# A two-layer mixer kernel on one core: the low parts of its weight blocks made by accumulating transfers

## The chip, the core and the metric

The kernel runs on one core of one Trainium2 chip. The metric is the time of one execution on the device, in microseconds (us). The kernel before has a median of 2033.26 us over two runs (2032.23 and 2034.3).

## What is computed

Two mixer layers work on 512 latent tokens and 256 context tokens with 1024 features. Each layer normalizes, scales and shifts its input, projects it with one wide weight matrix, runs two branches of eight heads (retention, and mLSTM with a matrix memory), merges them by sigmoid gates, projects once more and adds the result to its input. Cut to what matters here:

```
for l in range(DEPTH):
    hx = rmsnorm(x, norm_w) * (1 + sc_x) + sh_x            # hc the same way from ctx
    u  = einsum('bld,de->ble', h, w_in) + b_in             # rq rk rv rz mq mk mv mo mz mg gr gm
    br = einsum('ble,ed->bld', yr, w_ret_o)                # yr: head norm of retention, gated
    bm = einsum('ble,ed->bld', ym, w_ml_o)                 # ym: head norm of mLSTM, gated
    y  = sigmoid(gr) * br + sigmoid(gm) * bm
    x  = x + g_x * einsum('bld,de->ble', y, w_out)         # ctx too, in the first layer only
return rmsnorm(x, final_norm_w)
```

All weights and activations are float32. The second layer computes only the latent tokens behind its heads' keys and values.

## The kernel before

Activations lie transposed, features on the partitions and tokens on the free axis. Every large projection splits both operands into a high part, which is the value rounded to float32r, and a low part, which is the remainder, and sums three products in PSUM: high times high, high times low of the activation, and low of the weight times high. TensorE (PE) thus reads the low part of a weight block in every third matmul, the first of them being the third matmul of a group.

Weights come as blocks of 1024 by 128 numbers, kept as a tile of 128 partitions by 1024 numbers (512 KB). `specs` lists the units of work in order; a unit is two blocks, except for the unit `rvg` of each layer, which comes in three pieces. `wload` (L171) prepares a unit: for each block `rawtile` (L164) issues a load into one of three buffers of the tag `raw` on the queue of SP, and `split` (L160) writes the high part with ScalarE (ACT, L161) and the low part with VectorE (DVE, L162), which subtracts the high part from the raw block:

```
s.activation(dh, src, AF.Copy)
(eng or v).tensor_tensor(dl, src, dh.bitcast(F32), op=OP.subtract)
```

High and low parts lie in the tiles `wh` and `wl`, with two buffers each. `nextw` (L190) hands out the unit that is wanted and prepares the next one. A unit can be prepared only into the buffers of the unit before the one that PE works on, so its time is what PE needs for one unit. Both layers together have 124 units in 250 pieces: 121 pieces in the first layer, 129 in the second. `split` has other users, which the change leaves alone: the start parameters (`ada`), the normalized activations `h`, the branch results `yr`, `ym` and the merged `y`.

How long a unit lasts on PE depends on its place. In the first layer a unit of two blocks multiplies 512 latent and 256 context columns; in the second layer most multiply the 512 latent ones alone. The short units are these: in the output projection `ou` (L1081, `mm3`), which takes the tokens in two passes and loads all weights again for the second, the second pass of the first layer and both passes of the second handle 256 columns; and in the second layer the units `mv` (L980, `mvc`) of the mLSTM heads handle the 256 context tokens, each between a unit `mz` and the unit `vo` of an odd head (1, 3, 5, 7).

GpSimd (POOL) does elementwise work and issues a few stores: the rope sum (L654), products with row tables (L695, L822, L806), small fills (L762, L772, L781 to L785), a power for each norm (L377, L623), squares and products of the norms (L366, L386), and the stores of `yrd`, `ymd` (L636) and `gmd` (L996) to DRAM. The kernel is built with a scheduler that orders the instructions of each engine by its own estimate of times; every engine then runs its list in that order and waits at each instruction for what it needs.

Of the kernel before, what the change touches and what calls it, by code (L numbers as in the profile page):

```python
"""Two mixer layers (bidirectional retention and mLSTM branches) on one core.

Activations are kept transposed (features on partitions, tokens on the free axis,
context tokens first).  The large projections split each float32 operand into a
float32r part and its float32r remainder and sum three products in PSUM; the
attention products run in plain float32.
"""
# [1 line left out]

# [7 lines left out]
AF = mybir.ActivationFunctionType  # L17
OP = mybir.AluOpType
PSUM = bass.MemoryType.PSUM
# [40 lines left out]
def build(tc, io):  # L60
# [3 lines left out]
    with ExitStack() as es:  # L64
# [10 lines left out]
        v, s, g, pe = nc.vector, nc.scalar, nc.gpsimd, nc.tensor  # L75

        def stage(name, dt=F32):
            return stp.tile([P, 774], dt, tag="st", bufs=6, name=name)
# [10 lines left out]
        def chunks(t, n=NCH):  # L89
            return t.rearrange("p (n c) -> p n c", n=n)  # L90

        # Work units are emitted in order; after each, every generator under way
        # gives up one stage, so that what a stage needs is ready when it comes.
        main, side = [], []

        def advance(q, gen):
# [24 lines left out]
                yield  # L121
            yield from gen

# [1 line left out]
        def const(name, shape):  # L125
            t = cst.tile(list(shape), F32, name="k_" + name)
            nc.sync.dma_start(t, io[name])
            return t
# [27 lines left out]
        nhalf = cst.tile([P, 1], F32, name="nhalf")  # L156
        g.memset(nhalf, -0.5)

# [1 line left out]
        def split(dh, dl, src, eng=None):  # L160
            s.activation(dh, src, AF.Copy)  # L161
            (eng or v).tensor_tensor(dl, src, dh.bitcast(F32), op=OP.subtract)  # L162

        def rawtile(src, name, shape=(KB, P)):  # L164
            raw = wp.tile([P, KB * P], F32, tag="raw", bufs=3, name="raw_" + name)
            raw = raw[:, :shape[0] * shape[1]].rearrange("p (k c) -> p k c", k=shape[0])
            nc.sync.dma_start(raw, src)
            return raw

        specs, loaded, wpos = [], {}, [0]  # L170
        def wload(i):  # L171
            if i >= len(specs) or i in loaded:
                return
            name, blocks = specs[i]
            wh = wp.tile([P, KB * VG], F32R, tag="wh", bufs=2, name="wh_" + name)
            wl = wp.tile([P, KB * VG], F32R, tag="wl", bufs=2, name="wl_" + name)
            if name.startswith("rvg"):
                wh, wl = [t.rearrange("p (k c) -> p k c", k=KB) for t in (wh, wl)]
                for a, b in ((0, 3), (3, 6), (6, 8)):
                    raw = rawtile(blocks[0][:, a:b], f"{name}_{a}", (b - a, VG))  # L180
                    split(wh[:, a:b], wl[:, a:b], raw)
                loaded[i] = (wh, wl)
                return
            wh, wl = [t[:, :2 * KB * P].rearrange("p (j k c) -> p j k c", j=2, k=KB) for t in (wh, wl)]
            for j, ap in enumerate(blocks):
                raw = rawtile(ap, f"{name}_{j}")
                split(wh[:, j], wl[:, j], raw)
            loaded[i] = (wh, wl)

        def nextw(ahead=True):  # L190
# [49 lines left out]
                              start=kb == 0 and sx is hp[0] and mv is w[0], stop=kb == KB - 1 and mv is w[1])  # L240
            return ps

# [1 line left out]
        sil = cst.tile([P, KB, 2], F32, name="sil")  # L244
        s.activation(sil, ccols, AF.Tanh, scale=0.5)
        v.scalar_tensor_tensor(sil, sil, 1.0, ccols, op0=OP.add, op1=OP.mult)
# [49 lines left out]
        def ada_first(kb):  # L296
            w = loaded["a", kb]
            ps = btile(f"ada_{kb}")
            if kb in NATSET:
                for j in range(2):  # L300
                    for k in range(KB):
                        pe.matmul(ps[:, j * P:(j + 1) * P], sils[:, k].bitcast(F32), w[j][:, k], start=k == 0,
                                  stop=k == KB - 1)
            else:
                for mv in w:
                    for k in range(KB):
                        pe.matmul(ps[:, :2 * P], sils[:, k], mv[:, :, k], start=k == 0 and mv is w[0],
                                  stop=k == KB - 1 and mv is w[1])
            return ps
# [47 lines left out]
                    accs[i] = acc  # L357
                yield

# [1 line left out]
        def square_add(acc, xk, k, sl, eng=None):  # L361
            t = stage(f"sq{k}") if k else acc
            if eng is None:
                s.activation(t[:, sl], xk[:, sl], AF.Square)
            else:
                eng.tensor_tensor(t[:, sl], xk[:, sl], xk[:, sl], op=OP.mult)  # L366
            if k:
                v.tensor_tensor(acc[:, sl], acc[:, sl], t[:, sl], op=OP.add)
# [28 lines left out]
                s.activation(t[:, sl], t[:, sl], AF.Identity, scale=sc, bias=b)  # L397
            split(hi, lo, t[:, sl], v if l else g)

# [1 line left out]
        wb = io["wblk"]  # L401

        def spec(name, *blocks):
# [24 lines left out]
                for p in range(4):  # L428
                    spec(f"{nm}{p}_{l}", io[nm][l, 2 * p], io[nm][l, 2 * p + 1])

# [1 line left out]
        rst = stage("rst_in")  # L432
        acc = stage("acc_in")
        hp = (big.tile([P, KB, T], F32R, tag="b0", name="h0_hi"), big.tile([P, KB, T], F32R, tag="b1", name="h0_lo"))
# [1 line left out]
        rows = {0: ada_first(0)}  # L436
# [41 lines left out]
        for l in range(NL):  # L478
# [29 lines left out]
            ymd = [dr.tile([P, T], F32, name=f"ymd{l}_{h}") for h in range(H)]  # L508
            gmd = [dr.tile([P, T], F32, name=f"gmd{l}_{j}") for j in range(KB)]

# [1 line left out]
            def gates(gtok):  # L512
                for a, b in ((0, 4), (4, 6)):
                    ps = btile(f"gtr{l}_{a}")
# [87 lines left out]
            def gate_rows(h):  # L602
                nc.sync.dma_start(gw[:, :, qsl], grow[h:h + 1][:, :, qsl].to_broadcast([P, 4, qsl.stop - qsl.start]))

# [1 line left out]
            def gate_z(pss, j, vb, hb, zT, name):  # L606
                t = stage(name)
                for ps, sl in pss:
                    s.activation(t[:, sl], ps, AF.Tanh, scale=0.5, bias=hv[:, hb + j:hb + j + 1])
                    s.activation(zT[:, sl], ps, AF.Identity, bias=vc[:, vb + j:vb + j + 1])  # L610
                v.scalar_tensor_tensor(zT[:, qsl], t[:, qsl], 1.0, zT[:, qsl], op0=OP.add, op1=OP.mult)
# [28 lines left out]
                nc.sync.dma_start(bt, io["brow"][l, idx:idx + 1, :].to_broadcast([P, VG]))  # L640
                return bt

# [1 line left out]
            def ret_v(w, bt, p, n0):  # L644
                vt = chunks(vts[p % 2][:, :1536])
                ps = projv(w, hp, n0, f"rv{l}_{p}_{n0}")
                v.tensor_tensor(vt[:, n0:n0 + 2], chunks(ps, 2), bt[:, None, :256].to_broadcast([P, 2, 256]), op=OP.add)
# [104 lines left out]
                finished.add(("r", l, h))  # L752
                yield

# [1 line left out]
            def ml_v(w, bt, h, n0):  # L756
                vt = chunks(vts[h % 2])
                ps = projv(w, hp, n0, f"mv{l}_{h}_{n0}")
# [131 lines left out]
                finished.add(("m", l, h))  # L890
                yield

# [1 line left out]
            if l == 0:  # L894
                late_consts()
            zet = sml.tile([P, 2, H], F32, tag="zet", bufs=1, name=f"zet{l}")
# [1 line left out]
            for p in range(4):  # L898
# [43 lines left out]
                for i in range(6):  # L942
                    h = 2 * p + i // 3
# [38 lines left out]
                main.append(ml_att(h))  # L982
                tick(False)

# [1 line left out]
            if l == 0:  # L986
                side.append(ada_rest(gw, ada_todo[ADAN:]))
            for p in range(4):
                w = nextw()
                for jj in range(2):  # L990
                    j = 2 * p + jj
# [17 lines left out]
            for p in range(4):  # L1009
                w = nextw()  # L1010
                for jj in range(2):
                    j = 2 * p + jj
# [5 lines left out]
                    tick(False)  # L1018
            drain(main)

# [1 line left out]
            for p in range(4):  # L1022
                w = nextw()
                for jj in range(2):
                    j = 2 * p + jj
# [10 lines left out]
            for p in range(4):  # L1036
                w = nextw()
                for jj in range(2):
                    j = 2 * p + jj
# [6 lines left out]
                    tick()  # L1046
            drain(side)

# [1 line left out]
            X = big.tile([P, KB, T], F32, tag="b2", name=f"X{l}")  # L1050
            for j in range(KB):
                nc.sync.dma_start(X[:, j, qsl], (io["xT"][j] if l == 0 else x1d[j])[:, qsl])
# [19 lines left out]
            for i, sl in enumerate((LAT, CTX) if need else (slice(256, 512), slice(512, 768))):  # L1072
                n = sl.stop - sl.start
                d = 1 if sl is CTX else 0
                for p in range(4):
                    w = nextw()
                    for jj in range(2):
                        j = 2 * p + jj
# [87 lines left out]
```

## Time and profile before

| what | value |
|---|---|
| median of the runs, lowest, highest | 2033.26 us, 2032.23 us, 2034.3 us |
| span of the profiled execution, first to last instruction | 2032.1 us |
| PE busy | 1990.1 us, 98% of the span |
| DVE busy | 1427.0 us, 70% |
| ACT busy | 718.9 us, 35% |
| POOL busy | 370.0 us, 18% |
| bytes moved by DMA | 229.59 MB, 113 GB/s in the mean |

The span of the profiled execution lies 1.2 us below the median of the runs. Busy times are times in which an engine works; matmuls are pipelined, so that a new one can start long before the one before it ends, and two starts 0.12 us apart are possible with matmuls of 0.28 us. Instructions that issue a transfer are not counted as busy time.

### The profile page before, as it was taken

How to read it: one execution, taken by the hardware profiler on the slowest of the kernel's cores; microseconds unless marked ns; L12 is line 12 of the kernel's file. 1: busy time of each engine (PE TensorE's matmuls, PEld its weight loads, DVE VectorE, ACT ScalarE, POOL GpSimd, SP SyncE). 2: the span in 40 equal slices, each digit the busy share in tenths (PEclk: the TensorE clock that was granted, in tenths of full speed). 3: DMA queues.
4: the chain of work that ended last, by engine and by line, in shares of the span. 5: the costliest groups of instructions: out<-in, count | busy, mean ns of one | idle time of the engine just before them, and what ended most of it. 6: DMA issues, size and time to landing. Idle time of an engine off the chain costs nothing.

```text
span 2032.1 us, 32593 instructions
## 1 busy us (share of the span) xinstructions
PE 1990.1 (98%) x12676; PEld 1799.9 (89%) x12676; DVE 1427.0 (70%) x3303; ACT 718.9 (35%) x1362; POOL 370.0 (18%) x431
## 2 busy tenths in 40 slices
PE   6989999999999999999999999999999999999997
PEld 6988989999999999888888888899899999988887
DVE  7886996566858585888834689655667886763356
ACT  5423222334434434343212442322334444434223
POOL 4312222221212121100000341312212122110000
PEclk9999999999999999999999999999999999999999
DMA  8213322212322323454524431222233333325435
GB/s 297 75 45 104 123 81 84 71 57 101 106 82 88 100 85 98 162 175 153 175 86 158 152 101 45 96 71 76 76 112 103 117 120 121 114 98 184 137 120 171
DMA packets 74716, 229.59 MB, mean 113 GB/s; under 512 B 8960, under 2 KB 17408, under 8 KB 73536
## 3 DMA queue, kind: packets, MB, share of 16 engines
q1 hardware_dynamic: 70464, 211.56, 32.0%
q0 software_dynamic: 4096, 15.93, 2.0%
q8 instruction: 100, 1.64, 0.3%
q14 instruction: 56, 0.46, 0.1%
HBM read 206.29 MB, written 21.17 MB: 112 GB/s over the span
## 4 chain that ended last, share of the span: by engine, by line
PE 87%; DVE 9%; issue 2%; DMA 1%; ACT 0%; POOL 0%; SPq 0%; POOLq 0%; DVEq 0%; ACTq 0%
PE mv L232 11%; PE mqk_l L216 9%; PE rqk_l L216 7%; PE bm_l L216 4%; PE gm_l L216 4%; PE br_l L216 4%; PE mz_l L216 4%; PE gr_l L216 4%; PE rv L232 4%; PE ou L205 4%; PE mqk_c L218 3%; PE rz_l L216 3%; PE rqk_c L218 2%; PE ro L743 2%; PE mo L869 2%
## 5 line engine op out<-in xcount | busy, mean ns | idle before, releaser
L232 PE MATMUL mv<-wh_vo,h_hi 128*128 128x256 f32 x640 | 183.6, 287 | 0.0
L232 PE MATMUL mv<-wl_vo,h_hi 128*128 128x256 f32 x640 | 183.2, 286 | 0.0
L232 PE MATMUL mv<-wh_vo,h_lo 128*128 128x256 f32 x640 | 182.0, 284 | 0.0
L356 DVE SCALAR_TENSOR_TENSOR aacc<-gw,sil,aacc 128x128 f32<-128x128 f32 x448 | 138.7, 362 | 0.0
L232 PEld LDWEIGHTS mv<-wh_vo,h_hi 128*128 128x128 f32 x640 | 122.6, 191 | 0.4
L232 PEld LDWEIGHTS mv<-wh_vo,h_lo 128*128 128x128 f32 x640 | 122.5, 191 | 0.2
L792 DVE SCALAR_TENSOR_TENSOR cv<-u,vec,cv 128x770 f32<-128x770 f32 (+1 forms) x128 | 121.3, 949 | 1.8
L232 PEld LDWEIGHTS mv<-wl_vo,h_hi 128*128 128x128 f32 x640 | 122.4, 191 | 0.0
L822 POOL TENSOR_TENSOR ws<-ws,gw 128x768 f32<-128x768 f32 (+1 forms) x32 | 53.3, 1686 | 321.5 <-PE mo L871 155.1
L216 PE MATMUL mqk_l<-h_lo,wh_mqk 128*128 128x512 f32 x256 | 103.8, 405 | 0.0
L216 PE MATMUL mqk_l<-h_hi,wh_mqk 128*128 128x512 f32 x256 | 103.3, 403 | 0.0
L216 PE MATMUL mqk_l<-h_hi,wl_mqk 128*128 128x512 f32 x256 | 102.4, 400 | 0.0
L654 POOL TENSOR_TENSOR ws<-ws,rp 128x512 f32<-128x512 f32 x32 | 52.6, 1644 | 189.6 <-DVE ws L653 149.6
L232 PE MATMUL rv<-wl_rv,h_hi 128*128 128x256 f32 x288 | 83.2, 289 | 0.0
L232 PE MATMUL rv<-wh_rv,h_hi 128*128 128x256 f32 x288 | 83.1, 289 | 0.0
L232 PE MATMUL rv<-wh_rv,h_lo 128*128 128x256 f32 x288 | 82.8, 288 | 0.0
L205 PE MATMUL ou<-yl,wh_wout 128*128 128x256 f32 (+1 forms) x256 | 79.1, 310 | 0.0
L205 PE MATMUL ou<-yh,wl_wout 128*128 128x256 f32 (+1 forms) x256 | 79.1, 310 | 0.0
L205 PE MATMUL ou<-yh,wh_wout 128*128 128x256 f32 (+1 forms) x256 | 78.7, 309 | 0.0
L743 PE MATMUL ro<-ws,ws 128*128 128x128 f32 x448 | 65.2, 279 | 9.5 <-DVE gsm L563 3.9
L695 POOL TENSOR_TENSOR ws<-ws,ws 128x768 f32<-128x768 f32 (+1 forms) x32 | 53.1, 1678 | 106.4 <-PE ro L743 106.2
L743 PEld LDWEIGHTS ro<-ws,ws 128*128 128x128 f32 x448 | 59.7, 194 | 12.8 <-DVE st L744 8.1
(444 smaller groups left out, 6536.2 us busy)
## 6 DMA issues: line engine op xcount, KB each, us to landing
gw<-in_wada SPq DMA_DIRECT2D x32, 512.0 KB, 3.4
raw_vo<-in_wblk SPq DMA_DIRECT2D x32, 512.0 KB, 4.2
raw_mqk<-in_wblk SPq DMA_DIRECT2D x32, 512.0 KB, 3.8
raw_wout<-in_wout SPq DMA_DIRECT2D x32, 512.0 KB, 3.9
gw<-grow SPq DMA_DIRECT2D x8, 1536.0 KB, 6.3
raw_qk<-in_wblk SPq DMA_DIRECT2D x16, 512.0 KB, 3.4
raw_zq<-in_wblk SPq DMA_DIRECT2D x16, 512.0 KB, 3.3
raw_kz<-in_wblk SPq DMA_DIRECT2D x16, 512.0 KB, 3.7
```

What stands on the lines that cost most here:

```text
L205: pe.matmul(dst, lw[:, j, kb], mv[:, kb, sl], start=first, stop=last)
L216: pe.matmul(lat, lw[:, j, kb], mv[:, kb, LAT], start=first, stop=last)
L218: pe.matmul(c[:, :NCTX], lw[:, j, kb], mv[:, kb, CTX], start=first, stop=last)
L232: pe.matmul(dst, sx[:, kb, tk], mv[:, :, kb], start=first, stop=last)
L356: v.scalar_tensor_tensor(o, raw[:, kb], sil[:, kb, d:d + 1], o, op0=OP.mult, op1=OP.add)
L654: g.tensor_tensor(dst[:, LAT], dst[:, LAT], t[:, :512], op=OP.add)
L695: g.tensor_tensor(chunks(qd[d][:, qsl], nq), chunks(qT[:, qsl], nq), xi[d][:, None, :].to_broadcast([P, nq, P]), op=OP.mult)
L743: pe.matmul(o, lt, rt, start=k == 0, stop=k == len(ops) - 1)
L792: v.scalar_tensor_tensor(y[:, o0:o0 + n], u[:, o0 + i:o0 + i + n], cw[i], y[:, o0:o0 + n], op0=OP.mult, op1=OP.add)
L822: g.tensor_tensor(qd[d][:, qsl], qT[:, qsl], gw[:, 2 + d, qsl], op=OP.mult)
L869: pe.matmul(o, ch(sT[d], n), vt[:, n, 0:129], start=True, stop=first)
```

## The change

A new helper `wsplit` takes the place of `split` for the 250 weight pieces. ACT writes the high part as before, and then writes the negative of the raw block, rounded in the same way, into the low tile. POOL's queue then issues a transfer that reads the same weight block from DRAM a second time and adds it to what lies in the low tile: the block less its high part is the low part. DVE has no part in it any more. The raw load stays.

```
+        def wsplit(dh, dl, raw, src):
+
+            s.activation(dh, raw, AF.Copy)
+            s.activation(dl, raw, AF.Copy, scale=-1.0)
+            g.dma_start(dl, src, accum_op=OP.add)
...
                     raw = rawtile(blocks[0][:, a:b], f"{name}_{a}", (b - a, VG))
-                    split(wh[:, a:b], wl[:, a:b], raw)
+                    wsplit(wh[:, a:b], wl[:, a:b], raw, blocks[0][:, a:b])
...
                 raw = rawtile(ap, f"{name}_{j}")
-                split(wh[:, j], wl[:, j], raw)
+                wsplit(wh[:, j], wl[:, j], raw, ap)
```

The rest of the diff takes comments out; code below the helper stands six lines lower than before, so POOL's L623 is L629 in the changed kernel, L806 is L812, and the transfer of the helper is L168.

The scheduler orders the changed program anew. On POOL in the second layer's mLSTM heads, before, the stretch behind the power of head 1's norm (`ve_m1_1`) reads:

```order
L822 TENSOR_TENSOR ws3_1_11584<-ws1_1_11582,gw1_11585 128x512 x2
L772 MEMSET ws2_1_11583 128x2
L623 TENSOR_TENSOR ve_m1_1_15305<-ve_m1_1_15305,nhalf_104 128x4
L762 MEMSET ws2_1_11583 128x2
L781 MEMSET u1_3_0_15596 128x2
L782 MEMSET u1_3_0_15596 128x2
L636 DMA ymd1_1_11598<-yo_m1_1_15407 128x512
```

The same stretch of POOL's list in the changed kernel, where `wl_mv2`, `wl_vo3` and `wl_mqk3` are the low tiles of three units that follow each other:

```order
L168 DMA wl_mv2_1_15377<-in_wblk 128x1024 x2
L828 TENSOR_TENSOR ws3_1_11708<-ws1_1_11706,gw1_11709 128x512 x2
L629 TENSOR_TENSOR ve_m1_1_15479<-ve_m1_1_15479,nhalf_104 128x4
L168 DMA wl_vo3_1_15519<-in_wblk 128x1024 x2
L778 MEMSET ws2_1_11707 128x2
L787 MEMSET u1_3_0_15776 128x2
L788 MEMSET u1_3_0_15776 128x2
L812 TENSOR_TENSOR ws3_1_11708<-gw1_11709,k_negm_510 128x512
L168 DMA wl_mqk3_1_15624<-in_wblk 128x1024
```

The transfers for `wl_vo3` now stand behind the power of head 1's norm, and those for `wl_mqk3` behind that and a table product.

On PE in the second layer's output projection, where `ou1_4_0` and `ou1_5_0` belong to the unit `wout2` and `ou1_6_0` to the unit after it, the changed kernel reads as follows, behind the last matmul of the unit `wout1`:

```order
L211 MATMUL ou1_4_0_19182<-yh1_18723,wh_wout2_1_19100 128x256
L211 MATMUL ou1_4_0_19182<-yl1_18724,wh_wout2_1_19100 128x256
L211 MATMUL ou1_5_0_19211<-yh1_18723,wh_wout2_1_19100 128x256
L211 MATMUL ou1_5_0_19211<-yl1_18724,wh_wout2_1_19100 128x256
L211 MATMUL ou1_6_0_19252<-yh1_18723,wh_wout3_1_19170 128x256
L211 MATMUL ou1_6_0_19252<-yl1_18724,wh_wout3_1_19170 128x256
```

Before, the matmul that reads the low tile stood third in the list, and each block's 24 matmuls followed each other:

```order
L205 MATMUL ou1_4_0_18940<-yh1_18495,wh_wout2_1_18862 128x256
L205 MATMUL ou1_4_0_18940<-yl1_18496,wh_wout2_1_18862 128x256
L205 MATMUL ou1_4_0_18940<-yh1_18495,wl_wout2_1_18863 128x256
L205 MATMUL ou1_4_0_18940<-yh1_18495,wh_wout2_1_18862 128x256
L205 MATMUL ou1_4_0_18940<-yl1_18496,wh_wout2_1_18862 128x256
```

The first two matmuls of four blocks, which need high parts alone, are thus put ahead of the first that reads a low tile.

## Rows read from the trace of the kernel before

**Rows 1.** Page, part 1: busy us, share of the span, instructions.

```profile
span 2032.1 us, 32593 instructions
PE 1990.1 (98%) x12676; PEld 1799.9 (89%) x12676; DVE 1427.0 (70%) x3303; ACT 718.9 (35%) x1362; POOL 370.0 (18%) x431
```

**Rows 2.** Waits of PE, longest first: us in total, times, longest.

```profile
PE ada L307 <- ACT wh_ada L161: 8.1, 1, 8.1
PE ro L743 <- DVE gsm L563: 3.9, 1, 3.9
...
PE rkv L709 <- DVE adx L340: 0.6, 1, 0.6
PE rkv L709 <- ACT ws L618: 0.3, 1, 0.3
```

**Rows 3.** Windows by stage: us, busy by engine, PE clock, DMA share, GB/s.

```profile
1140.00:1170.00 30.00, 28.12 (x229) 27.69 (x228) 22.40 (x24) 16.69 (x23) 16.31 (x11) 0.99 0.54 163
1460.00:1790.00 330.00, 329.71 (x2205) 303.05 (x2205) 242.48 (x578) 136.14 (x275) 58.21 (x109) 1.00 0.35 111
1790.00:1962.00 172.00, 172.00 (x792) 143.24 (x791) 81.17 (x154) 58.08 (x87) 10.49 (x14) 1.00 0.44 144
1973.00:2020.00 47.00, 47.00 (x393) 46.87 (x391) 32.54 (x54) 20.77 (x31) 1.63 (x1) 1.00 0.57 191
```

**Rows 4.** Groups by line and shape: count | busy us, mean ns | idle before, releaser.

```profile
L162 DVE TENSOR_TENSOR wl_gr<-raw_gr,wh_gr 128x1024 fp32r<-128x1024 f32 x16 | 19.2, 1220 | 15.6 <-ACT wh_gr L161 15.6
...
L161 ACT ACTIVATE wh_gr<-raw_gr 128x1024 fp32r<-128x1024 f32 x16 | 16.0, 1050 | 20.9 <-PE gm_c L218 9.6 <-PE gm_l L216 5.1 <-PE gr_l L216 4.5
```

**Rows 5.** Tile wl_wout, 1962 to 2032 us: count, duration ns min/median/max, first and last start.

```profile
L205 PE MATMUL ou<-yh,wl_wout x128: 279/283/363, 1973.2 to 2019.8; 128*128 128x256 f32 x128
L162 DVE TENSOR_TENSOR wl_wout<-raw_wout,wh_wout x16: 1215/1220/1227, 1963.6 to 2011.3; 128x1024 fp32r<-128x1024 f32 x16
```

**Rows 6.** Tile wl_wro, 1876 to 1930 us.

```profile
L216 PE MATMUL br_l<-yrh,wl_wro x64: 389/389/389, 1886.4 to 1929.2; 128*128 128x512 f32 x64
```

**Rows 7.** DMA issues: count, KB each, median us from issue to landing.

```profile
raw_wout<-in_wout SPq DMA_DIRECT2D x32, 512.0 KB, 3.9
...
yrd<-yo_r POOLq DMA_DIRECT2D x8, 384.0 KB, 3.2
ymd<-yo_m POOLq DMA_DIRECT2D x8, 384.0 KB, 5.1
...
yrd<-yo_r POOLq DMA_DIRECT2D x8, 256.0 KB, 2.4
```

**Rows 8.** Page, part 3, DMA queues: packets, MB, share of 16 engines' span.

```profile
q1 hardware_dynamic: 70464, 211.56, 32.0%
q0 software_dynamic: 4096, 15.93, 2.0%
```

**Rows 9.** Tile wl_mz, 1550 to 1600 us.

```profile
L216 PE MATMUL mz_l<-h_hi,wl_mz x16: 389/394/481, 1570.3 to 1585.3; 128*128 128x512 f32 x16
```

**Rows 10.** Tile wl_vo, 1586 to 1606 us.

```profile
L232 PE MATMUL mv<-wl_vo,h_hi x32: 283/283/364, 1591.8 to 1604.7; 128*128 128x256 f32 x32
```

**Rows 11.** Timeline of POOL, 1580 to 1612 us: start, us, instruction [idle before, releaser].

```profile
1598.53 1.03 POOL L623 TENSOR_TENSOR ve_m<-ve_m,nhalf 128x4 f32<-128x4 f32 x1 [4.64 <-DVE ve_m L622]
...
1604.22 0.62 POOL L636 DMA_DIRECT2D ymd<-yo_m  x1 [4.53 <-DVE yo_m L634]
```

**Rows 12.** Timeline of POOL, 1140 to 1185 us.

```profile
1149.37 1.96 POOL L377 TENSOR_TENSOR rc_ms<-rc_ms,nhalf 128x4 f32<-128x4 f32 x1 [3.13 <-DMA x1d<-X]
...
1166.43 2.01 POOL L386 TENSOR_TENSOR xn<-X,rst 128x512 f32<-128x512 f32 x1 [0.36 <-DVE acc L368]
```

**Rows 13.** Tile wl_rvg, 1150 to 1200 us.

```profile
L239 PE MATMUL rvg<-wl_rvg,h_hi x46: 288/296/445, 1166.1 to 1199.7; 128*128 128x288 f32 x46
```

**Rows 14.** Timeline of POOL, 1196 to 1212 us.

```profile
1202.44 2.66 POOL L695 TENSOR_TENSOR ws<-ws,ws 128x512 f32<-128x512 f32 x2
```

**Rows 15.** Tile wl_zq, 1195 to 1220 us.

```profile
L216 PE MATMUL rz_l<-h_hi,wl_zq x8: 389/389/393, 1207.7 to 1212.5; 128*128 128x512 f32 x8
```

## The prediction

> **What bounds the kernel now.** I read the page's part 1 first: PE is busy for 98% of the span, DVE for 70%, ACT for 35%, POOL for 18% [rows 1]. Then the waits of PE: 16 rows that sum to 34.0 us. The first is the start, 8.1 us; the eleven that DVE ends run from 3.9 to 0.6 us and sum to 19.6 us [rows 2]. So PE's own pace is the bound, and nothing that DVE is spared can be worth more than about 20 us. The windows by stage say the same: PE is busy for all of 1460 to 1962 us and of the output projection behind it [rows 3]. The question is therefore less what DVE gains than whether the low tiles still come in time. For that I read, unit by unit, when PE stops reading a pair of buffers and when it reads the low part of the next unit in them. That distance is the time of one unit. In the last output projection 128 reads of `wl_wout` take 46.6 us for 8 units, 5.8 us each [rows 5]; in the branch output `br` 64 reads take 42.8 us for 4 units, 10.9 us each with the gap to the next counted [rows 6]; in the first layer, with 256 columns more a unit, it is longer.
>
> **What goes.** 250 subtractions of 1.22 us [rows 4] leave DVE, 305 us, 70% of the span down to about 55%. Of PE's waits on DVE those of the retention heads (3.9 us the longest) should shrink, those of the start and of the final norm stay. I take 10 us of the 19.6.
>
> **What comes.** ACT gets 250 copies more, 1.05 us each [rows 4], 262 us, which brings it to 48%. They wait for the same freed buffer as the high parts, and ACT's other work has room; beside the chain below I cost them at nothing. If ACT's list made PE's results wait for them, it would cost up to 2.1 us a unit, two copies more in a row. POOL gets 250 issues of about 0.62 us [rows 11], 155 us, 18% to 26% of the span. DMA gets 250 transfers more, 131 MB read.
>
> **The chain per unit.** Before, a low block follows the freed buffer by one copy and one subtraction, 1.05 + 1.22 us. In the changed kernel it takes two copies, the issue and the landing: 0.1 + 2 x 1.05 us and then A for a first block, two copies more for the second. A is the one number that no row shows, since no transfer of the kernel before accumulates. From below: a plain store from POOL lands in 2.4 us with 256 KB and in 3.2 us with 384 KB [rows 7], so plain 512 KB should take 4.0 us, and 3 us where nothing else runs. From above: an accumulating transfer reads its source and its destination and writes; if that went at a quarter of the plain rate it would be 10 us. For the time on the DMA engines, the plain rate is 325 GB/s (211.56 MB in 32.0% of the span) to 392 GB/s (15.93 MB in 2.0%) [rows 8], so 1.3 to 1.6 us for a block. Three streams where a copy has two make it 1.5 times that, about 2.3 us. For the landing I start from the nearest loaded row, `ymd` with 5.1 us for 384 KB [rows 7], since the raw loads of the next unit now come at the same moment, and add 0.8 us for the last 128 KB: A = 6 us. Both ends, 3 and 10 us, are kept for the range.
>
> The Trainium skill has a price for a transfer from POOL ("DMA: Bandwidth & Descriptors", Anatomy of one DMA — SWDGE (gpsimd) path): 2.0 us plus the bytes over 436 GB/s, which estimates 3.2 us here. The stores of 2.4 and 3.2 us agree with it, `ymd` with 5.1 us doesn't [rows 7]. By the fit, the low end of A would hold, and the sum would be the first rival's.
>
> With A = 6 us a first block is ready 8.2 us after the buffer is free and a whole unit 10.3 us. In units of 10.9 us and more this stays hidden. The places where it does not:
>
> 1. The last output projection. A unit takes 5.8 us; by the chain two buffers turn over in 8.2 + 5.8 us, 7.0 us a unit. By the DMA engines a unit needs 2 x 1.6 us raw and 2 x 2.3 us accumulated, 7.8 us; the stage already keeps them 57% busy with 191 GB/s [rows 3]. 2.0 us for each of seven units: 14 us. PE's new order, with the first two matmuls of four blocks ahead of the first low one, spares 0.5 us a unit at most and adds a wait for the next unit's high part; I cost it at nothing.
>
> 2. The end of the first layer. POOL's list now has the transfers of `wl_wout3` and of `wl_rvg` behind the products `xn`, one after the other: the sixth ends at 1168.4 us [rows 12], so the first low piece of `rvg` could land at 1168.4 + 0.6 + 6 = 1175 us, where PE reads it at 1166.1 us [rows 13]. That is 9 us, and the short units ahead of it add 3 us: 12 us. What queues behind those transfers on POOL are the last two `xn`, for which the new `h` waits.
>
> 3. The second layer's odd heads. PE reads the last of `wl_mz` at 1585.3 us and the first of `wl_vo` at 1591.8 us [rows 9, 10]; a whole unit takes 10.3 us, 4 us more. For head 3 POOL's list is worse: its transfers stand behind the power that ran from 1598.5 to 1599.6 us [rows 11], 8 us after PE's read. PE's own list moves head 1's products ahead, and DVE is quicker, so I count 7 us there, 5 us each for heads 5 and 7, 4 us for head 1, and 5 us for head 2, whose transfers stand behind table products in the same manner: 26 us. Behind a late transfer POOL's stores and table products wait too, and ACT's exponentials for these.
>
> 4. Smaller: the start, five issues of 0.62 us among POOL's products, 3 us; `wl_zq` of the second layer, behind a product that ends at 1205.1 us [rows 14], ready at about 1211 us where PE reads it at 1207.7 us [rows 15], 3 us.
>
> Sum: 14 + 12 + 26 + 3 + 3 - 10 = 48 us. On the profiled span of 2032.1 us this makes 2080 us, and with the 1.2 us by which the median of the runs lies above it, 2081 us, 2.4% slower. A change within 2% (2074 us) is about what a measurement of this kernel can't tell from none.
>
> **Rivals.** First, not slower: the transfers land like plain ones, A = 3 us. Its place is the short unit: the chain is then 5.2 us for a first block, less than 5.8, and the engines need 2 x 1.6 + 2 x 1.3 = 5.8 us; the odd heads lose 1 us each, POOL's order still costs 5 us at the layer's end and 5 us in the heads, the start 3 us, and DVE's 10 us come back: 2032 + 17 - 10 + 1 = 2040 us. It decides from about A = 5 us down. For it speak the stores of 2.4 us, against it that loads and transfers now come together. Second: the DMA engines become the bound. If an accumulated block costs four plain ones, 5.2 us on the engines, a unit needs 2 x 1.6 + 2 x 5.2 = 13.6 us with its raw loads. Then 16 units of 10.9 us in the second layer lose about 3 us each, 12 short ones 8 us each, the heads between 1460 and 1790 us, whose 24 units take 13.8 us each, about 1 us each, and the places of POOL's order 40 us: 48 + 96 + 24 + 40 - 10, about 200 us, 2230 us. For it speaks that the branch outputs already hold the engines at 44% [rows 3] with one load a block; against it, that it takes four times the plain price. Third: DVE's relief is all that counts, and every wait for DVE goes. That is 2013 us, 1% and inside the 2%; there is no place on PE for more.
>
> The Trainium skill has a rule against the change ("SBUF — State Buffer", SBUF: two separate sides, with its part A bandwidth-pool intuition that's wrong): transfers from GpSimd's queue need descriptors that it writes through a port that some DVE instructions hold, so that a small transfer of 0.62 us took 3.1 us. The issues of the kernel before take 0.62 us [rows 11] but their landings spread from 2.4 to 5.1 us [rows 7], which would fit. By this rule A would stay at 6 us or above for as long as DVE is busy, and the time be the forecast's or more.
>
> **Numbers.** Forecast, 2055 to 2115 us: 0.45. First rival, 2030 to 2055 us: 0.27. DMA-bound, 2115 to 2400 us: 0.23. Relief alone, 2010 to 2030 us: 0.05. The range for 8 in 10 reaches over most of the first rival and half of the second: 2036 to 2190 us. Slower by over 2%: 0.23 and most of the forecast's 0.45, 0.61. Within 2%: 0.37. Faster by over 2%: 0.02.
>
> **What would show it.** The issue list should show 250 accumulating transfers at about 6 us to landing; the second queue's share should rise from 2.0% to some 30%. PE's waits should name the transfers of `wl_wout` (about 14 us), of `wl_vo` and `wl_rvg`. DVE should be near 1120 us busy, ACT near 980. If PE's waits name only DVE and the start, or landings lie below 5 us, the forecast is wrong towards the first rival; if the DMA share is near 1 in the branch outputs, towards the second.

## The result, and the profile after

The changed kernel takes 2141.71 us (median of two runs, 2140.92 and 2142.5) where the kernel before takes 2033.26 us: a ratio of 1.0535 with a 95% interval of 1.0505 to 1.0566, 108 us slower. The forecast was slower by 48 us, with a range up to 2190 us: the direction was right, the size less than half.

Part 1 of the page of the changed kernel, which answers to [rows 1]:

```profile
span 2140.7 us, 32988 instructions
...
PE 2025.2 (95%) x12676; PEld 1824.1 (85%) x12676; DVE 1155.4 (54%) x3053; ACT 946.4 (44%) x1612; POOL 565.3 (26%) x681
```

DVE lost 272 us of work (305 were counted), ACT gained 228 (262) and POOL 195 (155). On POOL the instructions that issue a transfer do count as busy, as its 250 instructions more show (681 where it had 431). PE has the same 12676 matmuls and 35 us more of busy time. The waits of PE, longest first (us in total, times, longest), answer to [rows 2]:

```profile
PE ou L211 <- DMA wl_wout<-in_wout: 18.0, 10, 4.0
PE mv L238 <- DMA wl_vo<-in_wblk: 17.8, 4, 5.7
PE ou L211 <- ACT wh_wout L166: 12.5, 4, 7.6
PE ada L313 <- ACT wh_ada L161: 8.2, 1, 8.2
PE rz_l L222 <- DMA wl_zq<-in_wblk: 6.3, 2, 4.0
```

All 27 rows of this view sum to 106.9 us, where the 16 of before summed to 34.0. Those that name a transfer into a low tile sum to 55.8 us; those that name DVE to 17.4 us, where they were 19.6. So 73 us of the 108 are waits. The other 35 us are what the same matmuls took longer, and TensorE's clock fits nearly all of it: the view of the cores gives a mean granted clock of 0.978 over 2140.7 us, where it was 0.993 over 2032.1 us, 47 us of full clock not granted where it was 14. Windows of the changed kernel for its four late stages (us, busy time of PE, PEld, DVE, ACT and POOL, granted clock, DMA share, GB/s): the end of the first layer, the second layer's mLSTM heads, its gates and branch outputs, and the last output projection. They answer to [rows 3].

```profile
1101.00:1191.00 90.00, 77.95 (x409) 67.24 (x407) 21.82 (x34) 45.02 (x56) 27.94 (x30) 0.91 0.91 245
...
1475.00:1851.00 376.00, 348.71 (x2255) 318.99 (x2254) 206.47 (x548) 185.57 (x332) 103.68 (x161) 0.97 0.66 165
1851.00:2049.50 198.50, 188.14 (x840) 153.65 (x839) 52.20 (x123) 90.89 (x123) 39.00 (x46) 0.98 0.83 212
2049.50:2132.50 83.00, 58.87 (x402) 56.50 (x400) 18.91 (x43) 34.30 (x46) 13.54 (x16) 0.84 0.80 202
```

PE stands idle in the heads and in the output projection, where it had hardly a gap before. The DMA engines are busy for 66 to 91% of these stages, where the heads had 35%, the branch outputs 44% and the output projection 57%. The page's queues (packets, MB, share of 16 engines) and its issues (KB each, median us to landing) say why; they answer to [rows 7, 8].

```profile
q0 software_dynamic: 40096, 146.23, 34.7%
q1 hardware_dynamic: 70464, 211.56, 30.1%
...
raw_vo<-in_wblk SPq DMA_DIRECT2D x32, 512.0 KB, 7.6
wl_vo<-in_wblk POOLq DMA_DIRECT2D x32, 512.0 KB, 9.5
raw_wout<-in_wout SPq DMA_DIRECT2D x32, 512.0 KB, 8.7
wl_wout<-in_wout POOLq DMA_DIRECT2D x32, 512.0 KB, 9.0
...
X<-x1d SPq DMA_DIRECT2D x8, 256.0 KB, 13.7
```

The forecast's unknown, the landing A, is 9 to 10 us and not 6. The share of q0 rose by 32.7% of the span, 700 us or 2.8 us a block; the forecast had 2.3. Plain loads suffer too: the raw loads of the output projection went from 3.9 to 8.7 us.

Where the time went is read from the last matmul of a unit's tiles in the two traces. The table says how much later it starts than in the kernel before, stage by stage (us gained or lost in the stage, and, rounded apart, the sum), for the changed kernel and for runs that are explained below.

| stage, last unit | changed | plain | second_only | dve_add | three_low | raw2_st5 |
|---|---|---|---|---|---|---|
| first layer, start and retention, kz3 | -2.6 | -1.9 | -0.4 | +1.5 | +6.6 | +2.3 |
| mLSTM heads, mqk7 | +1.5 | +1.6 | +0.1 | +2.1 | +4.1 | +1.6 |
| gates, branch outputs, wmo3 | +4.8 | -1.3 | +0.6 | -1.0 | +0.4 | +1.5 |
| output projection, wout3 | +21.3 | +9.0 | +6.7 | 0.0 | +14.2 | +25.2 |
| second layer, its start and retention, kz3 | -5.9 | -8.5 | -2.2 | +5.1 | +10.1 | +4.9 |
| mLSTM heads, mqk7 | +41.8 | +20.9 | +7.8 | +0.4 | +2.5 | +33.7 |
| gates, branch outputs, wmo3 | +15.6 | 0.0 | +2.0 | 0.0 | +13.3 | +21.7 |
| output projection, wout3 | +31.2 | +16.0 | +15.8 | +4.5 | +39.8 | +30.8 |
| sum | +107.8 | +35.8 | +30.3 | +12.6 | +91.0 | +121.6 |

One odd head shows the chain whole. Timelines of ACT, POOL and PE in head 3 of the second layer (start, us, instruction, idle time before it and what ended it):

```profile
1620.74 1.99 ACT L166 ACTIVATE wh_vo<-raw_vo 128x1024 fp32r<-128x1024 f32 x2
1622.64 0.68 ACT L615 ACTIVATE mzt<-mz_l,hvec 128x512 f32<-128x512 f32 x1
1623.21 0.69 ACT L616 ACTIVATE ws<-mz_l,vec 128x512 f32<-128x512 f32 x1
1623.78 2.01 ACT L167 ACTIVATE wl_vo<-raw_vo 128x1024 fp32r<-128x1024 f32 x2
...
1622.39 1.04 POOL L629 TENSOR_TENSOR ve_m<-ve_m,nhalf 128x4 f32<-128x4 f32 x1 [5.32 <-DVE ve_m L628]
1625.13 1.82 POOL L168 DMA_DIRECT2D wl_vo<-in_wblk  x2 [1.71 <-ACT wl_vo L167]
...
1637.57 0.39 PE L238 MATMUL mv<-wl_vo,h_hi 128*128 128x256 f32 x1 [4.36 <-DMA wl_vo<-in_wblk]
```

ACT's copies end at 1625.8 us, both high parts and two of its other instructions first; POOL's second issue begins at 1626.1 us, and PE goes on at 1637.6 us, 11.5 us later. POOL's power, which stands ahead of these transfers in its list, had ended 1.7 us before the first issue and delayed nothing.

### The profile page after: what moved, and what is told of

Read it like the earlier page. It is cut to its first block, busy times and chain, and to the rows that moved or that the text cites. A ratio compares the mean times of both kernels' runs of the same rounds, so it can differ in the third digit from the quotient of the medians.

```text
span 2140.7 us, 32988 instructions
## 1 busy us (share of the span) xinstructions
PE 2025.2 (95%) x12676; PEld 1824.1 (85%) x12676; DVE 1155.4 (54%) x3053; ACT 946.4 (44%) x1612; POOL 565.3 (26%) x681
## 5 line engine op out<-in xcount | busy, mean ns | idle before, releaser
L211 PE MATMUL ou<-yh,wl_wout 128*128 128x256 f32 (+1 forms) x256 | 85.5, 339 | 18.0 <-DMA wl_wout<-in_wout 18.0
L211 PE MATMUL ou<-yh,wh_wout 128*128 128x256 f32 (+1 forms) x256 | 85.2, 335 | 14.2 <-ACT wh_wout L166 12.5
L660 POOL TENSOR_TENSOR ws<-ws,rp 128x512 f32<-128x512 f32 x32 | 45.2, 1413 | 184.9 <-DVE ws L659 184.9
L211 PE MATMUL ou<-yl,wh_wout 128*128 128x256 f32 (+1 forms) x256 | 84.9, 333 | 0.0
L766 DVE TENSOR_TENSOR ws<-mv,br_mv 128x512 f32<-128x512 f32 x40 | 27.5, 686 | 100.3 <-PE mv L238 100.3
L800 ACT ACTIVATE u<-cv 128x770 f32<-128x770 f32 (+1 forms) x32 | 25.4, 795 | 114.0 <-DVE cv L798 108.7
L211 PEld LDWEIGHTS ou<-yh,wl_wout 128*128 128x128 f32 x256 | 54.4, 214 | 23.3 <-DMA wl_wout<-in_wout 20.3
```

The source lines that it names most:

```text
L211: pe.matmul(dst, lw[:, j, kb], mv[:, kb, sl], start=first, stop=last)
L660: g.tensor_tensor(dst[:, LAT], dst[:, LAT], t[:, :512], op=OP.add)
L766: v.tensor_tensor(o, ps.rearrange("p (n a b) -> p n a b", n=2, a=2), bt[:, :256].rearrange("p (a b) -> p a b", a=2)[:, None].to_broadcast( ...
L800: s.activation(u[:, o0:o0 + n], y[:, o0:o0 + n], AF.Tanh, scale=0.5)
```

## The experiments

All ratios are to the kernel before on the same chip, 2031.7 to 2032.0 us.

**A tail that measures the transfer.** Behind the last result of the kernel before:

```
for r in rs: s.activation(r, X, Copy); nc.sync.dma_start(r, wb[1, 8 + k])
for t in ts: s.activation(t, X, Copy, scale=-1.0); g.dma_start(t, wb[1, k], accum_op=OP.add)   # or plain
```

> The kernel before with a tail behind its last result: transfers of one weight block (512 KB) from GpSimd's queue into the buffers of the low parts, four times each, plain and accumulating, one alone, two together, and two together with two raw loads from SyncE's queue. Theory 1 (the accumulation itself is slow: each packet takes twice as long and nothing else is needed to explain the landing): one plain 3.5 to 4.5 us to landing, one accumulating 6 to 7 us; two together 5 and 9 us; with two raw loads 7 and 10 to 11 us. Theory 2 (the landing of 9.5 us is made by the other work of the kernel, DVE's hold on GpSimd's descriptors or the order of the lists): one accumulating below 5 us, two below 6 us, and with two raw loads below 8 us, since DVE is idle here.

The tail missed its aim: the raw loads ran far ahead of the groups that they belonged to and fell beside the single transfers, and ACT's copies kept the pairs 2.7 us apart. What it gives is the pairs with nothing else in flight: 3.5 to 3.7 us plain, 5.4 us accumulating, with or without a neighbour 2.7 us away. So 6 to 7 us for one alone was too high, and below 5 us too low.

**The accumulation alone: plain.** The transfer keeps its place, bytes and queue, and leaves the whole block in the low tile in place of the low part.

```
-            g.dma_start(dl, src, accum_op=OP.add)
+            g.dma_start(dl, src)
```

> The changed kernel with the accumulation taken off its 250 transfers: they overwrite the low tile with the whole block, so the low part of each weight is left out and the product with it is wrong; same bytes, same queue, same copies and almost the same lists. Theory 1 (the accumulation makes the transfer late): landing 5 to 7 us in place of 9.5, q0 at about 17% in place of 34.7%, time 2045 to 2075 us. Theory 2 (the order of the lists and the two copies on ACT make it late, whatever the transfer does): 2110 to 2145 us. Theory 3 (a second read of every block from DRAM is what fills the DMA engines): landing 8 us or more and 2095 us or more.

2069.85 us, ratio 1.0191 (1.0175 to 1.0207). Queue and issues of its page:

```profile
q0 software_dynamic: 40096, 146.23, 20.1%
...
wl_vo<-in_wblk POOLq DMA_DIRECT2D x32, 512.0 KB, 6.2
...
raw_wout<-in_wout SPq DMA_DIRECT2D x32, 512.0 KB, 5.5
wl_wout<-in_wout POOLq DMA_DIRECT2D x32, 512.0 KB, 6.6
```

Theory 1 holds: 72 of the 110 us hang on the accumulation. A second read of every block, with its copies on ACT and its issues on POOL, costs the other 38 us. Theory 2 (lists) and theory 3 (the second read as such) would have left over 2095 us.

**ACT's copies alone: dve_add.**

```
-            g.dma_start(dl, src, accum_op=OP.add)
+            v.tensor_tensor(dl, raw, dl.bitcast(F32), op=OP.add)
```

> The changed kernel with VectorE adding the raw block to the negated high part in place of the transfer: ACT has both its copies, DVE its 250 operations of about 1.2 us as before, DMA and POOL what they had before. Theories 1 and 3: 2030 to 2045 us, at most 12 us over before, for 1.05 us more in the chain of each block. Theory 2 (ACT's second copy and its list delay the high parts and PE's results): 2070 us or more, with PE's waits naming ACT.

2046.21 us, 1.0066 (1.0051 to 1.0081): 14 us, a little over the bound of 12 and the range up to 2045. The table puts 5 us of it at the start of the second layer and 4.5 us in the last output projection. ACT's second copy is a small cause.

**Half of the transfers: second_only.**

```
-                wsplit(wh[:, j], wl[:, j], raw, ap)
+                if j:
+                    wsplit(wh[:, j], wl[:, j], raw, ap)
+                else:
+                    split(wh[:, j], wl[:, j], raw)
```

> The changed kernel with the accumulating transfer for the second block of each unit alone; the first block and the three pieces of rvg's first use are as before for the first block, and as in the changed kernel for rvg. The second block's low part is read half a unit later than the first, 2.9 us in the short units and 5.3 us in the branch outputs. Theory 1 (chain per unit of copy, copy, issue and landing against the time of a unit): a landing of about 7 us alone, hidden in the branch outputs, 1 to 2 us late in each short unit: 2050 to 2070 us. Theory 3 (the DMA engines' time): half the added engine time, about half the loss: 2080 to 2095 us.

2062.83 us, 1.0149 (1.0133 to 1.0166), as theory 1 had it. With 128 of the 250 transfers under a third of the loss is left (31 of 110 us), so it doesn't go with the engines' time alone. A transfer lands in 8.0 us in the median, where 7 were expected. The run changes two things at once: half of the accumulated bytes are gone, and each transfer that is left has half a unit more to land. The waits of PE:

```profile
PE ou L214 <- DMA wl_wout<-in_wout: 13.3, 5, 4.7
...
PE mv L241 <- DMA wl_vo<-in_wblk: 4.2, 4, 2.6
```

**A third low buffer: three_low**, with its control raw2_st5, which has the first two edits alone. The rest of the edit keeps the low part of rvg in two tiles, in four pieces.

```
-            raw = wp.tile([P, KB * P], F32, tag="raw", bufs=3, ...)
+            raw = wp.tile([P, KB * P], F32, tag="raw", bufs=2, ...)
-            return stp.tile([P, 774], dt, tag="st", bufs=6, name=name)
+            return stp.tile([P, 774], dt, tag="st", bufs=5, name=name)
-            wl = wp.tile([P, KB * VG], F32R, tag="wl", bufs=2, ...)
+            wl = wp.tile([P, 2 * KB * P], F32R, tag="wl", bufs=3, ...)
...
```

> The changed kernel with a third buffer for the low parts, paid for by one raw buffer (two in place of three) and one stage buffer (five in place of six); the low part of rvg is kept in two tiles. The low tile of a unit can then be made while PE works on the unit two before it. Theory 1a (what is lost is the delay from copy to landing, which one unit's time doesn't cover): the odd heads of the second layer (38 us lost) and its branch outputs (16 us) come back; the last output projection keeps what the DMA engines need, 2 raw and 2 accumulated blocks in 8.6 us against 5.8: 2055 to 2090 us. Theory 3 (the DMA engines' time is the bound everywhere it is lost): 2115 us or more.

> The changed kernel with two raw buffers and five stage buffers, as the run with three low buffers has them, and two low buffers as before: what the smaller buffers cost alone. Both theories: 2142 to 2165 us.

The control took 2155.47 us, 1.0605 (1.0586 to 1.0625). With the third buffer it was 2125.93 us, 1.0464 (1.0450 to 1.0478): 30 us better than the control, but a total that theory 3 had named and theory 1a had not. The stages tell more. Issues and the window of the mLSTM heads, with the third low buffer:

```profile
wl_vo<-in_wblk POOLq DMA_DIRECT2D x32, 512.0 KB, 5.8
...
raw_wout<-in_wout SPq DMA_DIRECT2D x32, 512.0 KB, 7.8
...
1475.00:1850.00 375.00, 373.23 (x2437) 339.58 (x2436) 225.54 (x592) 204.34 (x362) 117.31 (x177) 1.00 0.75 181
```

In the heads PE is busy for all but 2 us, and 31 of the control's 33.7 us are gone, while the DMA engines are busier (0.75) than in the changed kernel (0.66). There the loss was delay and not the engines' time. The delay itself is shorter: of the 14 transfers of `wl_vo` for heads 1 to 7 of the second layer, each had a raw load issued within 1 us of it in the changed kernel and landed in 7.8 to 11.5 us; with the third buffer none had one within 2.5 us, and they landed in 5.2 to 6.8 us. In the gates and branch outputs, where theory 1a had all of it come back, 13.3 of 21.7 us stayed. In the last output projection nothing came back, 9 us more were lost: a unit's raw loads wait for two raw buffers, as in the control, land in about 8 us, and only then can the copies and the transfers follow, one behind the other. Whether a third low buffer with all raw buffers would help there wasn't tried.

**Squares on DVE: sq_dve.**

```
-                        square_add(acc, X[:, j], j, sl, g if sl is CTX else None)
+                        square_add(acc, X[:, j], j, sl, g if sl is CTX else None if need else v)
```

> The changed kernel with the squares of the second layer's output projection on DVE in place of ACT. In the changed kernel PE waits 12.5 us there for high parts of wl_wout's units, and on ACT's list squares that wait for PE's results stand ahead of these copies. If that is the cause, 8 to 12 us come back: 2129 to 2135 us. If the raw loads (landing in 8.7 us) make the high parts late, nothing changes: 2138 to 2144 us.

2143.92 us, 1.0551 (1.0536 to 1.0565), no gain: the squares on ACT's list are not the cause. Most of the waits for high parts stayed (9.6 of 12.5 us):

```profile
PE ou L211 <- ACT wh_wout L166: 9.6, 4, 4.4
```

**PE's order: ou_near.** In the changed kernel the longest wait for a high part, 7.6 us, is one of the matmuls that PE's new order puts ahead: it belongs to `wout3`, while the low part of `wout2` behind it had landed. That wait ended with a raw load: issued at 2064.5 us beside the reloads of `X`, it landed at 2077.0 us, 12.4 us later, and ACT's copy and PE followed at once.

```
-                        tag = ("lat", "ctx")[j % 2]
+                        tag = ("lat", "ctx")[j % 2] if need else "lat"
```

> The changed kernel with one PSUM tag in place of two for the second layer's output projection: PE can put the first two matmuls of two blocks, not of four, ahead of a low part. In the changed kernel PE stood for 7.6 us at a high part of the unit wout3 while the low part of wout2, behind it in its list, had landed (2071.3 us; read at 2078.7 us). If PE's new order makes this wait, 6 to 10 us come back there: 2131 to 2136 us. If only the late raw loads and transfers of the stage count, and PE would wait for the next low part instead: 2139 to 2144 us.

2147.19 us, 1.0567 (1.0549 to 1.0585): nothing came back. PE's waits in that stage no longer name a high part, but others; behind them the reload of `X` in this run:

```profile
PE ou L211 <- DMA wl_wout<-in_wout: 15.1, 5, 6.6
PE ou L211 <- DVE X L1088: 11.4, 2, 10.2
...
X<-x1d SPq DMA_DIRECT2D x8, 256.0 KB, 15.3
```

The second one is for a result that DVE can't add, since `X` is late: its reload takes 15.3 us (5.9 us before, 13.7 us in the changed kernel). With one PSUM tag PE has fewer places for results and so waits for DVE; the run does not show what PE's order costs by itself. Neither this, nor the squares, nor a third low buffer paid for with a raw one sped up the last output projection. Each time another of its transfers ends last: raw blocks, low blocks or `X`, the plain ones more than twice as long in flight as before. What helped took load off the DMA engines: leaving the accumulation away (16 us lost in place of 31) or half of the transfers (15.8 us). The engines' time points the same way. Window of the same stage in the run plain:

```profile
1992.00:2055.50 63.50, 52.55 (x396) 50.57 (x395) 18.05 (x40) 33.71 (x45) 8.17 (x15) 0.92 0.74 257
```

Shared among eight units, 0.74 of 63.5 us is 5.9 us of the engines for each, where PE needs 5.8. In the changed kernel 0.80 of 83.0 us, in the window shown above, is 8.3 us. The 2.5 us over make 20 of the 31 us lost. How the rest divides between the chain, the late raw loads and the clock stays open.

**Where the unit is long: long_only, and where DVE was waited for: ret_only.**

```
+                if LONG(name):
                     wsplit(wh[:, j], wl[:, j], raw, ap)
+                else:
+                    split(wh[:, j], wl[:, j], raw)
```

> Accumulating transfers for the first layer's units up to its gate gm alone, where PE needs 17 to 22 us a unit; all later units are as before. In the changed kernel these units were never late but for one (zq, 2.3 us), and PE reached the unit vo0 2.6 us earlier than before. Theory 1 (a transfer that lands within the unit's time costs nothing, and DVE's relief is worth 2 to 3 us): 2028 to 2032 us against 2032. If a lighter DVE is worth nothing: 2032 to 2036 us.

> Accumulating transfers only for the units rv, qk, zq and kz of the retention heads 2 to 7 in both layers (24 units, 48 of the 250 pieces); all others as before. In the changed kernel PE made up 5.5 us between the units kz0 and rv1 of the first layer and 4.0 us between rv1 and qk1 of the second, where before it waited for DVE. If a lighter DVE is what gives that back: 2024 to 2029 us against 2032. If it was only time lost just ahead that came back: 2031 to 2036 us.

long_only took 2034.67 us, 1.0011 (1.0002 to 1.0020), and ret_only 2030.5 us, 0.9993 (0.9984 to 1.0002). ret_only fell between its two ranges. Transfers in units of 17 us cost about 2 us in all, and a lighter DVE gives back nothing that can be told from no change. In long_only the first layer loses 3.4 us at the start and makes as much up right behind it. No version was found that beats the kernel before.

**The transfer in groups.** The tail again, with one instruction of DVE that releases all transfers of a group at once, and a last kind in which DVE then works for about 13 us:

```
v.tensor_scalar(dum, ...)          # reads all tiles of the group's copies
for t in ts: g.dma_start(t, wb[1, k + i], accum_op=OP.add)
for r in rs: nc.sync.dma_start(r, wb[1, 8 + k + i])
for i in range(work): v.scalar_tensor_tensor(busy, X[:, 0:2], dum, X[:, 2:4], op0=OP.mult, op1=OP.add)
```

> The kernel before with a tail behind its last result: groups of transfers of one block each, all released by one instruction of DVE, four groups of each kind: one and two from GpSimd's queue, plain and accumulating, two with two raw loads from SyncE's queue, and two accumulating ones while DVE works on float32 tiles. The first tail, where the transfers came 2.7 us apart, had 3.5 us plain and 5.4 accumulating. Theory 1b (an accumulating transfer lands in 5.4 us alone; the rest of the 9.5 us is time on the DMA engines, shared with its neighbour and the raw loads): two accumulating 6.5 to 7.5 and 8 to 8.5 us; with two raw loads 8.5 to 9.5 and 10.5 to 11.5, and the raw loads 8 us or more; plain with raw loads 6 to 7. With DVE at work as without, within 0.5 us. Theory 2b (DVE keeps GpSimd from writing descriptors): with raw loads below 8 us, with DVE at work 9 us or more.

Each kind by its tile: count, duration of the issue in ns, first and last start, and under it the landing from issue in us, least, median and most.

```profile
L1115 POOL DMA_DIRECT2D plone<-in_wblk x4: 537/540/587, 2021.9 to 2040.6; - x4
...
DMA to landing us min/median/max: 3.5/3.6/3.8
...
L1113 POOL DMA_DIRECT2D actwo<-in_wblk x8: 858/1040/1234, 2103.7 to 2135.3; - x8
...
DMA to landing us min/median/max: 5.4/6.4/7.5
...
L1115 POOL DMA_DIRECT2D plmix<-in_wblk x8: 537/538/576, 2144.9 to 2176.7; - x8
...
DMA to landing us min/median/max: 5.2/6.3/7.4
...
L1113 POOL DMA_DIRECT2D acmix<-in_wblk x8: 854/1036/1221, 2186.3 to 2224.3; - x8
...
DMA to landing us min/median/max: 7.6/9.0/10.4
...
L1113 POOL DMA_DIRECT2D acdve<-in_wblk x8: 854/880/1221, 2237.0 to 2276.3; - x8
...
DMA to landing us min/median/max: 5.2/5.9/8.5
```

Each group has two landings. Two accumulating transfers land after 5.4 and 7.4 us; with two raw loads beside them after 7.7 and 10.3 us, and plain ones with raw loads after 5.3 and 7.3 us. That is nearly the changed kernel's landing (9.0 us in the median for the first block of a unit, 10.8 us for the second), made with nothing but four transfers. With DVE at work the median is no higher than without (5.9 against 6.4 us); one transfer of the eight took 8.5 us. So the landing is made by the transfers that go together, as theory 1b had it, though its figures for two accumulating ones were too high (6.5 and 8 us at least, and 8.5 and 10.5 with raw loads). Theory 2b falls for the DVE instruction tried; a copy or another one was not tried. Without any DVE work the four transfers come within 1.3 us of the landing in the changed kernel, so little is left for it.

## Why the prediction was wrong

**The step that failed is "add 0.8 us for the last 128 KB: A = 6 us".** A is the issue to the landing. With nothing beside it, it is 5.4 us; with the unit's other block and the raw loads of the next unit, which ACT's copies release at the same moment, 7.7 and 10.3 us. The row from which A was worked out, a store with 5.1 us, was a plain transfer, and the time that an accumulated block adds on the engines (2.8 us, where 1.3 to 1.6 us were set for a plain one) was put into a separate sum, the engines' time per unit, and not into A, where the four transfers queue for each other. The plain transfers of the experiment land in 6.2 us (`wl_vo`) and 6.6 us (`wl_wout`), and that kernel loses 38 us: the forecast priced about that kernel.

The sum with the measured terms comes nearer. The forecast's 14 us for the last output projection came from the engines' time (7.8 us a unit), so there the term that failed is the 2.3 us: with 2.8 us a unit needs 2 x 1.6 + 2 x 2.8 = 8.8 us, 3.0 us over, 21 us for seven units. By the chain a first block takes 0.1 + 3 x 1.05 us (ACT writes both high parts first), 0.3 us to the issue and, in this stage, 8.0 us in the median to land, 11.6 us: (11.6 + 5.8) / 2 is 8.7 us a unit, 20 us for seven. 31.2 us were lost; the low clock and the late raw loads are in neither sum. In the odd heads a whole unit takes 0.1 + 4 x 1.05 + 0.3 + 10.8 us, 15.4 us where the forecast had 10.3; 26 us were forecast, 41.8 lost. The branch outputs were called hidden, since 8.2 us are less than 10.9. With 9.0 us, the median landing of all first blocks, the chain is 12.6 us, which is more. 15.6 us were lost there and in the gates ahead of them, some 8 us of these in one unit of `gr` whose raw loads were late, and between 5 and 6 us in the branch outputs themselves.

**The clock was left out.** Of 108 us some 33 are clock, a term that the forecast did not have. Windows around the wait of head 3 shown above, in the changed kernel (a DMA share can pass 1, since the view counts a packet's whole time where it starts):

```profile
1633.00:1637.50 4.50, 0.21 (x2) 0.01 (x1) 2.84 (x8) 2.22 (x9) 2.47 (x4) 1.00 1.06 252
...
1638.40:1641.80 3.40, 3.40 (x19) 3.40 (x18) 0.00 (x0) 0.00 (x0) 0.00 (x0) 0.50 1.04 323
```

PE stood still for 4.4 us, and 0.8 us after it went on the granted clock was at half, 1.2 GHz in place of 2.4, for 3.4 us. Its timeline shows the step from one matmul to the next go from 0.12 to 0.21 us:

```profile
1638.03 0.28 PE L238 MATMUL mv<-wl_vo,h_hi 128*128 128x256 f32 x1
1638.15 0.28 PE L238 MATMUL mv<-wh_vo,h_hi 128*128 128x256 f32 x1
...
1638.59 0.41 PE L238 MATMUL mv<-wh_vo,h_hi 128*128 128x256 f32 x1
1638.80 0.41 PE L238 MATMUL mv<-wh_vo,h_lo 128*128 128x256 f32 x1
```

The forecast counted each wait once; with what follows, the added waits cost about 1.5 times their length (108 over 73 us).

**POOL's list cost little.** The forecast's 12 us at the first layer's end rested on transfers that stand behind the products `xn`. ACT's copies and POOL's issues there:

```profile
1173.60 1.99 ACT L167 ACTIVATE wl_wout<-raw_wout 128x1024 fp32r<-128x1024 f32 x2
...
1180.28 1.72 ACT L167 ACTIVATE wl_rvg<-raw_rvg 128x864 fp32r<-128x864 f32 x2
...
1175.41 1.78 POOL L168 DMA_DIRECT2D wl_wout<-in_wout  x2
...
1182.16 1.74 POOL L168 DMA_DIRECT2D wl_rvg<-in_wrvg  x2
```

The issues follow the copies within 1 us. The whole list cost no transfer more than 3.1 us, and half of them 0.3 us. The place was right (14 us are lost from the first layer's `wmo3` up to the second layer's `qk0`), the 12 us came near by luck, and the cause was the landing. The 7 and 5 us for heads 3 and 2 rested on POOL's list too. By the last matmul of each head's unit `vo`, head 3 lost 9.3 us, no more than heads 5 and 7 (9.3 and 9.7 us) and less than head 1 (14.2 us), and head 2 lost nothing.

**DVE's relief was not 10 us.** Its waits went from 19.6 to 17.4 us, and the two runs with transfers only where units are long or DVE was waited for stand at 1.0011 and 0.9993. The longest wait of before, 3.9 us for `gsm`, is gone, but PE now waits longer for `st` (4.1 us in place of 3.3), `ws` and others.

**The rivals.** The first (A = 3 us) was wrong; with nothing else in flight a plain transfer of 512 KB already takes 3.6 us and an accumulating one 5.4 us. The second had the sign of the branch outputs right, a DMA share of 0.83, but an accumulated block costs about two plain ones on the engines and not four: 2.8 us, where the share of q0 in the run plain (20.1%) gives 1.5 us. The Trainium skill's fit ("DMA: Bandwidth & Descriptors", Anatomy of one DMA — SWDGE (gpsimd) path), 3.2 us by the estimate, is near the plain transfer alone, 3.6 us; for the accumulating one the trace has 5.4 us. The Trainium skill's rule that some DVE instructions hold up the descriptors ("SBUF — State Buffer", SBUF: two separate sides, with its part A bandwidth-pool intuition that's wrong) names a copy for its figure of 3.1 us, and no experiment here sets a copy beside a transfer; with the `scalar_tensor_tensor` that was tried, two transfers landed in 5.9 us in the median, without it in 6.4 us.

## What to carry to other kernels

A transfer that takes over an elementwise step is to be priced by its landing among the transfers that are released with it, not by its landing alone: list what the same event sets free, and queue all of it. Such a step is free only where a buffer's turn is longer than copies, issue and landing together, here 12 to 15 us; where it is shorter, each unit pays, and an engine that had no gaps pays once more with its clock. Work taken off an engine comes back only as far as the waits that name it shrink: 272 us less on DVE took 2.2 us off them.

## What was not expected of the hardware

An accumulating transfer with 4 KB packets took 327 ns a packet on its DMA engine where plain ones from SyncE's queue took 161, and its issue on POOL 0.86 us where a plain one took 0.54. Raw loads that go beside accumulating transfers are late too: in the groups of the last experiment the second of two landed after 8.6 us beside accumulating transfers and after 7.3 us beside plain ones, where the quickest `raw_wout` of the kernel before took 3.1 us. Even a reload of 256 KB from SyncE's queue went from 5.9 to 13.7 us.
